# Two of the first loads on ScalarE's queue, small rows behind them, and the first norm shared between two engines

## Chip, cores and metric

One core of a Trainium2 chip runs the whole kernel. The metric is the device time of one execution in microseconds; lower is better.

## The reference, cut to what matters

A trunk of two layers on 256 tokens of width 1024, all in f32. Each layer norms x, modulates it by a vector made from `c`, projects it with `w_in`, runs two groups of attention heads, projects back and adds.

```python
cs = jax.nn.silu(c)
for l in range(DEPTH):                                   # DEPTH = 2
    mod = cs @ w_ada[l] + b_ada[l]                       # 1024 x 3072
    shift, scale, gate = split(mod, 3)
    h = rmsnorm(x, g_pre[l]) * (1.0 + scale) + shift     # x: 256 x 1024
    y = hybrid_mixer(h, w_in[l], w_out[l], ...)          # h @ w_in: 1024 x 3864
    x = x + gate * rmsnorm(y, g_post[l])

def rmsnorm(x, g):
    return x * lax.rsqrt(jnp.mean(x * x, axis=-1, keepdims=True) + 1e-6) * g
```

## The kernel before

x lies in two tiles `x[0]` and `x[1]` of 128 tokens by 1024 ("first half" and "second half" here). The first layer starts in an order written out by hand (`first_layer_start`, L793), behind which a scheduler orders the rest from `PLAN`. The start runs in five stages over the rows of the weights: `STAGES` gives for each the first block of 128 rows and how many (1, 1, 2, 2, 2). A stage needs the shift and scale of its rows, so it loads its own columns of `w_ada` and multiplies them with silu(c) on TensorE (`ada_on_pe`, L217), takes them out through ScalarE (`accr`, L246), turns them back (L253) and adds `b_ada` (`ada_cols`, L260). Then VectorE modulates x's transpose (L875), ScalarE and VectorE split it into a high and a low part (`hH` L878, `hL` L879), do the same with the weights (`hi` L365, `lo` L373), and TensorE multiplies three times for f32 (L858, L400 to L402).

The pieces of `w_ada` lie in tiles that are named for what they hold later: in stage 0 `qm` holds the 128 columns of shift and `km` those of scale, 512 KB each; then `qs`, `yH`, `yL` and again `qm`, `km`, `qs`, `yH`, `yL`. The weights of `w_in` lie in `raw`, a pool of seven buffers. All loads are issued on SP's queue in the order of the code. A load has one of eight semaphores in turn, and waits until the load eight places before it has landed.

x's way to the first projection: `square` on ScalarE with a sum beside it, in two halves of 512 columns (L310); `rstd` adds the two sums on VectorE (L304) and takes the power -0.5 on GpSimd (L306); `xhat_scale` multiplies on VectorE (L323), into a tile named `z` for the first half and `modG` for the second; TensorE transposes (`xt`, L832). On TensorE stand, in this order: matmuls with the identity (`warm`, L284, no part of the result), four transposes of `z`, `qm`'s matmuls, four transposes of `modG`, the transpose of the small rows `modrows` (`b_ada`, `g_pre`, `g_post`, L182), `km`'s matmuls.

Of the kernel before, what the change touches and what calls it, by code (L numbers as in the profile page):

```python
# [12 lines left out]
AF = mybir.ActivationFunctionType  # L13
OP = mybir.AluOpType
# [3 lines left out]
P = 128  # L18
S = 256
D = 1024  # L20
NT = S // P
# [47 lines left out]
class Trunk:  # L69
# [78 lines left out]
    def load_x_c(self):  # L148
        nc = self.nc
        self.c8 = self.cp.tile([KK, P], F32, name="c8")  # L150
        nc.sync.dma_start(self.c8, self.I["c"][0].rearrange("(k p) -> k p", p=P))
        self.x = []
        for t in range(NT):
            xt = self.cp.tile([P, D], F32, name=f"x{t}")
            nc.sync.dma_start(xt, self.I["x"][0, t * P:(t + 1) * P, :])
            self.x.append(xt)

    def silu_c(self):
# [27 lines left out]
        self.mb = mc  # L186
        self.mod = self.tl(self.mp, [P, 24], "mod", bufs=2)

    def ada_loads(self, l, spec, slots=None):

        wv = self.I["w_ada"][l].rearrange("(k p) c -> p k c", p=P)
        nk = UNIT // (spec[0][2] * P)
        units = []
        for u in range(KK // nk):
            for part, k0, n in spec:
                if slots:
                    raw = slots[len(units)].rearrange("p (k c) -> p k c", k=nk)
                else:
                    raw = self.tl(self.rp, [P, nk, n * P], "raw")
                c0 = part * D + k0 * P  # L200
                self.nc.sync.dma_start(raw, wv[:, u * nk:(u + 1) * nk, c0:c0 + n * P])
                units.append(raw)
        return units

# [588 lines left out]
    def first_layer_start(self):  # L793

        nc = self.nc
        l = 0
        wv = self.I["w_in"][l].rearrange("(k p) c -> p k c", p=P)
        tags = [("qm", 1), ("km", 1), ("qs0", 1), ("qs1", 1), ("yH", 2), ("yL", 2)]
        tags += tags
        spec = [[(0, k, n), (1, k, n)] for k, n in STAGES]  # L800

        def loads(s):
            k, n = STAGES[s]
            slots = []
            while len(slots) < 2 * n:
                tag, m = tags.pop(0)
                t = self.tl(self.mp, [P, m, UNIT], tag)
                slots += [t[:, i] for i in range(m)]
            ada = self.ada_loads(l, spec[s], slots)
            ks = slice(k, k + n)  # L810
            cols = [self.COLS_A0, [(O_KC, O_KS + 128), (O_KW, O_KW + 128)],
                    [(O_QN, O_QN + 512)], [(O_ZN, O_ZN + 256)]]
            return ada, [self.load([wv[:, ks, a:b] for a, b in c], n, sum(b - a for a, b in c))
                         for c in cols]

        self.load_mod_rows(0)
        ua, uw = loads(0)
        self.warm(WARM[0])
        self.silu_c()
        self.warm(WARM[1])  # L820
        xT = [self.tl(self.tp, [P, 4, S], "wide") for _ in range(2)]
        sq = [self.xhat_square(t, self.mp, ("z", "modG")[t]) for t in range(NT)]
        xh = [self.xhat_scale(t, h, self.rstd(ssq[:, 0:1], ssq[:, 1:2]))
              for t, (h, ssq) in enumerate(sq)]
        self.start_layer()
        pm = self.tl(self.ps, [P, 512], "av", bufs=1)

# [42 lines left out]
        for s, (k0, n) in enumerate(STAGES):  # L870
# [10 lines left out]
            if s + 1 < len(STAGES):  # L881
                ua, uw = loads(s + 1)
                on_dve = ON_VECTOR[s]
                if on_dve:
                    acc = self.ada_on_dve(spec[s + 1], ua[:on_dve])
# [166 lines left out]
```

## Time and profile before

| | |
|---|---|
| three timed runs, us | 343.06, 345.75, 345.78 (median 345.75) |
| profiled execution, us | 344.3, of which the span 342.6 |
| TensorE busy | 327.5 us, 96% |
| VectorE, ScalarE busy | 77%, 59% |

The span runs from the first to the last instruction that the profiler recorded. Busy shares are means over stages with different limits; the start of the kernel, where the change is, has to be read by itself.

### The profile page before, as it was taken

How to read it: one execution, taken by the hardware profiler on the slowest of the kernel's cores; microseconds unless marked ns; L12 is line 12 of the kernel's file. 1: busy time of each engine (PE TensorE's matmuls, PEld its weight loads, DVE VectorE, ACT ScalarE, POOL GpSimd, SP SyncE). 2: the span in 40 equal slices, each digit the busy share in tenths (PEclk: the TensorE clock that was granted, in tenths of full speed). 3: DMA queues.
4: the chain of work that ended last, by engine and by line, in shares of the span. 5: the costliest groups of instructions: out<-in, count | busy, mean ns of one | idle time of the engine just before them, and what ended most of it. 6: DMA issues, size and time to landing. Idle time of an engine off the chain costs nothing.

```text
span 342.6 us, 7585 instructions
## 1 busy us (share of the span) xinstructions
PE 327.5 (96%) x2852; PEld 294.5 (86%) x2852; DVE 264.8 (77%) x727; ACT 203.0 (59%) x506; POOL 10.2 (3%) x23
## 2 busy tenths in 40 slices
PE   8899989989999999989998999999999999999993
PEld 7689979989988887868998899998989889877992
DVE  2647686999998997878999968699899654796232
ACT  4423315866788985749376527471599935698311
POOL 2000000300000000000020100000000000000000
PEclk9999999999999999999999999999999999999999
DMA  7999999829985657699967698749557540000111
GB/s 236 317 319 355 349 346 262 237 64 330 348 275 182 223 191 239 196 312 371 284 173 226 184 200 243 214 166 346 185 162 260 194 125 0 2 0 3 64 62 61
DMA packets 72060, 71.12 MB, mean 208 GB/s; under 512 B 11440, under 2 KB 61784, under 8 KB 72024
## 3 DMA queue, kind: packets, MB, share of 16 engines
q1 hardware_dynamic: 72024, 70.65, 66.5%
q8 instruction: 22, 0.36, 0.4%
q14 instruction: 14, 0.11, 0.1%
HBM read 69.58 MB, written 1.06 MB: 206 GB/s over the span
## 4 chain that ended last, share of the span: by engine, by line
PE 68%; DVE 15%; DMA 8%; issue 4%; ACT 2%; POOL 1%; SPq 1%; DVEq 0%; POOLq 0%; ACTq 0%
PE pj L400 14%; PE pj L401 13%; PE pj L402 13%; PE tr L569 5%; DVE lo L373 4%; PE av L622 3%; DMA yL<-in_w_ada_dram 3%; PE tr L217 2%; PE sc L636 2%; DMA km<-in_w_ada_dram 2%; PE sc L604 2%; PE sc L605 2%; PE pj L858 2%; PE av L647 2%; DMA raw<-in_w_in_dram 2%
## 5 line engine op out<-in xcount | busy, mean ns | idle before, releaser
L373 DVE TENSOR_TENSOR lo<-raw,hi 128x1024 fp32r<-128x1024 f32 (+3 forms) x82 | 90.6, 1124 | 14.1 <-ACT hi L365 13.8
L400 PE MATMUL pj<-hH,lo 128*128 128x256 f32 x320 | 92.2, 288 | 0.0
L401 PE MATMUL pj<-hL,hi 128*128 128x256 f32 x320 | 91.4, 286 | 0.0
L402 PE MATMUL pj<-hH,hi 128*128 128x256 f32 x320 | 91.3, 285 | 0.0
L365 ACT CAST hi<-raw 128x1024 fp32r<-128x1024 f32 (+4 forms) x70 | 66.2, 966 | 18.3 <-PE pj L402 15.6
L400 PEld LDWEIGHTS pj<-hH,lo 128*128 128x128 f32 x320 | 61.1, 191 | 3.1 <-issue 2.3
L401 PEld LDWEIGHTS pj<-hL,hi 128*128 128x128 f32 x320 | 61.1, 191 | 1.3 <-issue 0.7
L402 PEld LDWEIGHTS pj<-hH,hi 128*128 128x128 f32 x320 | 61.1, 191 | 1.1 <-issue 0.6
L549 ACT ACTIVATE S<-S,mn 128x128 f32<-128x128 f32 (+1 forms) x96 | 42.8, 449 | 2.9 <-DVE mn L546 2.8
L234 DVE SCALAR_TENSOR_TENSOR acc<-raw,cs,acc 128x512 f32<-128x512 f32 x49 | 36.4, 744 | 2.0 <-DMA raw<-in_w_ada_dram 1.7
L546 DVE CUSTOM_DVE_ANT_0 S<-sc,bias 128x128 f32<-128x128 f32 (+1 forms) x96 | 30.9, 350 | 4.4 <-PE tr L569 2.6
L400 PE MATMUL pj<-hi,yL 128*128 128x256 f32 x112 | 31.8, 287 | 0.0
L402 PE MATMUL pj<-hi,yH 128*128 128x256 f32 x112 | 31.8, 285 | 0.0
L401 PE MATMUL pj<-lo,yH 128*128 128x256 f32 x112 | 31.7, 284 | 0.0
L575 ACT COPY PT<-tr 128x384 f32<-128x384 f32 x44 | 19.9, 480 | 12.8 <-PE tr L569 12.5
L400 PEld LDWEIGHTS pj<-hi,yL 128*128 128x128 f32 x112 | 20.9, 188 | 1.5 <-issue 1.3
L569 PE MATMUL tr<-ident,S 128*128 128x128 f32 x144 | 21.9, 278 | 0.2
L401 PEld LDWEIGHTS pj<-lo,yH 128*128 128x128 f32 x112 | 21.0, 188 | 0.6 <-issue 0.6
L402 PEld LDWEIGHTS pj<-hi,yH 128*128 128x128 f32 x112 | 21.1, 188 | 0.4 <-issue 0.4
L557 ACT ACTIVATE S<-S,sm 128x256 f32<-128x256 f32 (+1 forms) x46 | 20.2, 482 | 1.7 <-DVE sm L553 1.4
L549 ACT ACTIVATION_READ_ACCUMULATOR S<-S,mn 128x1 f32 x96 | 18.3, 191 | 0.0
L246 ACT COPY accr<-tr 128x128 f32<-128x128 f32 x12 | 3.2, 265 | 25.4 <-PE tr L241 18.4
(242 smaller groups left out, 626.5 us busy)
## 6 DMA issues: line engine op xcount, KB each, us to landing
raw<-in_w_in_dram SPq DMA_DIRECT2D x43, 512.0 KB, 4.7
raw<-in_w_ada_dram SPq DMA_DIRECT2D x32, 512.0 KB, 4.7
raw<-in_w_out_dram SPq DMA_DIRECT2D x16, 512.0 KB, 9.1
raw<-in_w_in_dram SPq DMA_DIRECT2D x9, 256.0 KB, 5.2
qs<-in_w_ada_dram SPq DMA_DIRECT2D x4, 512.0 KB, 8.8
yH<-in_w_ada_dram SPq DMA_DIRECT2D x4, 512.0 KB, 7.9
yL<-in_w_ada_dram SPq DMA_DIRECT2D x4, 512.0 KB
raw<-in_w_in_dram SPq DMA_DIRECT2D x9, 128.0 KB, 5.6
```

What stands on the lines that cost most here:

```text
L234: nc.vector.scalar_tensor_tensor(out=out, in0=raw[:, j], scalar=self.cs[:, k:k + 1], in1=out, op0=OP.mult, op1=OP.add)
L365: self.nc.scalar.copy(hi[:, :nk * n], raw[:, :nk * n])
L373: self.nc.vector.tensor_sub(lo[:, :nk * n], raw[:, :nk * n], hi[:, :nk * n].bitcast(F32))
L400: nc.tensor.matmul(out, aL, bH, start=first, stop=False)
L401: nc.tensor.matmul(out, aH, bL, start=False, stop=False)
L402: nc.tensor.matmul(out, aH, bH, start=False, stop=last)
L546: nc.vector.tensor_tensor_reduce(out=s[:, a:b], in0=sc[:, a:b], in1=self.bias[:, h, S - (b - a):S], scale=-1.0, scalar=3.0e38, op0=OP.add, ...
L549: nc.scalar.activation(s[:, a:b], s[:, a:b], AF.Exp, bias=mn[:, i:i + 1], scale=-1.0, accum_out=sm[:, i:i + 1])
L557: nc.scalar.activation(s[:, a:b], s[:, a:b], AF.Copy, scale=sm[:, i:i + 1]))
L569: mms += [nc.tensor.transpose(pt[:, i * P:(i + 1) * P], blk, self.ident) for i, blk in enumerate(blocks)]
L575: self.copies.append(nc.scalar.copy(ps, pt[:, :3 * P]))
L622: mms.append(nc.tensor.matmul(av[j * HD:(j + 1) * HD, kt * P:S], self.vsw[:, kt, vc], pts[j][:, kt * S:S + kt * P], start=False, stop=(i = ...
```

## The change

x's first half and `qm` are issued on ScalarE's queue, ahead of ScalarE's first other work; x's second half and `km` stay on SP. The three loads of `modrows` move behind `km`. x's second half is squared and summed on VectorE while ScalarE does the first half, and is scaled on ScalarE in place of VectorE; both `rstd` stand behind the squares.

```diff
--- before.py
+++ after.py
@@ -152,7 +152,7 @@
         self.x = []
         for t in range(NT):
             xt = self.cp.tile([P, D], F32, name=f"x{t}")
-            nc.sync.dma_start(xt, self.I["x"][0, t * P:(t + 1) * P, :])
+            (nc.sync if t else nc.scalar).dma_start(xt, self.I["x"][0, t * P:(t + 1) * P, :])
             self.x.append(xt)
 
     def silu_c(self):
@@ -186,7 +186,7 @@
         self.mb = mc
         self.mod = self.tl(self.mp, [P, 24], "mod", bufs=2)
 
-    def ada_loads(self, l, spec, slots=None):
+    def ada_loads(self, l, spec, slots=None, queues=None):
 
         wv = self.I["w_ada"][l].rearrange("(k p) c -> p k c", p=P)
         nk = UNIT // (spec[0][2] * P)
@@ -198,7 +198,8 @@
                 else:
                     raw = self.tl(self.rp, [P, nk, n * P], "raw")
                 c0 = part * D + k0 * P
-                self.nc.sync.dma_start(raw, wv[:, u * nk:(u + 1) * nk, c0:c0 + n * P])
+                queue = queues[len(units)] if queues else self.nc.sync
+                queue.dma_start(raw, wv[:, u * nk:(u + 1) * nk, c0:c0 + n * P])
                 units.append(raw)
         return units
 
@@ -806,22 +807,35 @@
                 tag, m = tags.pop(0)
                 t = self.tl(self.mp, [P, m, UNIT], tag)
                 slots += [t[:, i] for i in range(m)]
-            ada = self.ada_loads(l, spec[s], slots)
+            ada = self.ada_loads(l, spec[s], slots, None if s else (nc.scalar, nc.sync))
+            if s == 0:
+                self.load_mod_rows(0)
             ks = slice(k, k + n)
             cols = [self.COLS_A0, [(O_KC, O_KS + 128), (O_KW, O_KW + 128)],
                     [(O_QN, O_QN + 512)], [(O_ZN, O_ZN + 256)]]
             return ada, [self.load([wv[:, ks, a:b] for a, b in c], n, sum(b - a for a, b in c))
                          for c in cols]
 
-        self.load_mod_rows(0)
         ua, uw = loads(0)
         self.warm(WARM[0])
         self.silu_c()
         self.warm(WARM[1])
         xT = [self.tl(self.tp, [P, 4, S], "wide") for _ in range(2)]
-        sq = [self.xhat_square(t, self.mp, ("z", "modG")[t]) for t in range(NT)]
-        xh = [self.xhat_scale(t, h, self.rstd(ssq[:, 0:1], ssq[:, 1:2]))
-              for t, (h, ssq) in enumerate(sq)]
+        sq = [(self.tl(self.mp, [P, D], tag), self.tl(self.sp, [P, 2], "ssq"))
+              for tag in ("z", "modG")]
+        for half in range(2):
+            cs = slice(half * 512, (half + 1) * 512)
+            (h0, ssq0), (h1, ssq1) = sq
+            self.square(h0[:, cs], self.x[0][:, cs], ssq0[:, half:half + 1])
+            nc.vector.scalar_tensor_tensor(out=h1[:, cs], in0=self.x[1][:, cs], scalar=1.0 / D,
+                                           in1=self.x[1][:, cs], op0=OP.mult, op1=OP.mult,
+                                           accum_out=ssq1[:, half:half + 1])
+        rs = [self.rstd(ssq[:, 0:1], ssq[:, 1:2]) for h, ssq in sq]
+        xh = [h for h, ssq in sq]
+        self.xhat_scale(0, xh[0], rs[0])
+        for half in range(2):
+            cs = slice(half * 512, (half + 1) * 512)
+            nc.scalar.activation(xh[1][:, cs], self.x[1][:, cs], AF.Copy, scale=rs[1])
         self.start_layer()
         pm = self.tl(self.ps, [P, 512], "av", bufs=1)
 
```

On SP's queue, from the first load on, before (`c`, x, the small rows, `w_ada`, then `w_in`; a bracket names the semaphore that is waited for):

```order
L151 DMA c_95<-in_c_dram 8x128
L155 DMA x_97<-in_x_dram 128x1024
L155 DMA x_99<-in_x_dram 128x1024
L175 DMA modrows_104<-in_b_ada_dram 24x128
L175 DMA modrows_104<-in_g_pre_dram 8x128
L175 DMA modrows_104<-in_g_post_dram 8x128
L201 DMA qm_108<-in_w_ada_dram 128x8x128
L201 DMA km_109<-in_w_ada_dram 128x8x128
L357 DMA raw_112<-in_w_in_dram 128x128 [waits DMAHW0_49]
L357 DMA raw_112<-in_w_in_dram 128x152 [waits DMAHW1_49]
L357 DMA raw_112<-in_w_in_dram 128x232 [waits DMAHW2_49]
L357 DMA raw_116<-in_w_in_dram 128x384 [waits DMAHW3_49]
```

and now:

```order
L151 DMA c_95<-in_c_dram 8x128
L155 DMA x_99<-in_x_dram 128x1024
L202 DMA km_105<-in_w_ada_dram 128x8x128
L175 DMA modrows_108<-in_b_ada_dram 24x128
L175 DMA modrows_108<-in_g_pre_dram 8x128
L175 DMA modrows_108<-in_g_post_dram 8x128
L358 DMA raw_112<-in_w_in_dram 128x128 [waits DMAHW0_49]
L358 DMA raw_112<-in_w_in_dram 128x152 [waits DMAHW1_49]
L358 DMA raw_112<-in_w_in_dram 128x232 [waits DMAHW2_49]
L358 DMA raw_116<-in_w_in_dram 128x384 [waits DMAHW3_49]
L358 DMA raw_116<-in_w_in_dram 128x128 [waits DMAHW4_49]
L358 DMA raw_119<-in_w_in_dram 128x512 [waits DMAHW5_49]
```

`x_97` and `qm` are gone to ScalarE, and the small rows stand behind `km`. The loads of TensorE's first tiles show which load has which semaphore: now x's first half 0, `c` 1, x's second half 2, `qm` 3, `km` 4, the small rows 5 to 7; so the first `raw_116` waits for `qm` and the second for `km`, where before they waited for two of the small rows.

On SP's queue a little later, at the end of stage 1's weights (`raw_250` to `raw_259`) and the start of stage 2, before:

```order
L357 DMA raw_250<-in_w_in_dram 128x232 [waits DMAHW3_49]
L357 DMA raw_254<-in_w_in_dram 128x384 [waits DMAHW4_49]
L357 DMA raw_254<-in_w_in_dram 128x128 [waits DMAHW5_49]
L357 DMA raw_257<-in_w_in_dram 128x512 [waits DMAHW6_49]
L357 DMA raw_259<-in_w_in_dram 128x256 [waits DMAHW7_49,DVE_49,Activation_49]
L201 DMA yH_354<-in_w_ada_dram 128x4x256 [waits DMAHW0_49]
L201 DMA yH_354<-in_w_ada_dram 128x4x256 [waits DMAHW1_49]
L201 DMA yL_355<-in_w_ada_dram 128x4x256 [waits DMAHW2_49]
L201 DMA yL_355<-in_w_ada_dram 128x4x256 [waits DMAHW3_49]
```

and now, with loads that belong to the compression of the keys further on (`pe`, `w`):

```order
L358 DMA raw_250<-in_w_in_dram 128x232 [waits DMAHW3_49]
L358 DMA raw_254<-in_w_in_dram 128x384 [waits DMAHW4_49]
L358 DMA raw_254<-in_w_in_dram 128x128 [waits DMAHW5_49]
L358 DMA raw_257<-in_w_in_dram 128x512 [waits DMAHW6_49]
L436 DMA pe_892<-in_pe_k_dram 16x128 [waits DMAHW7_49]
L436 DMA pe_892<-in_pe_v_dram 16x128 [waits DMAHW0_49]
L465 DMA w_147_991<-in_w_ck_dram 64x64 [waits DMAHW1_49]
L466 DMA w_147_991<-in_w_ck_dram 64x64 [waits DMAHW2_49]
L467 DMA w_147_991<-in_w_cv_dram 64x64 [waits DMAHW3_49]
L358 DMA raw_259<-in_w_in_dram 128x256 [waits DMAHW4_49,DVE_49,Activation_49]
L202 DMA yH_354<-in_w_ada_dram 128x4x256 [waits DMAHW5_49]
L202 DMA yH_354<-in_w_ada_dram 128x4x256 [waits DMAHW6_49]
```

Five small loads, which stood some thirty places further back, have moved ahead of `raw_259` and `yH`, and `yH` waits for other loads than before.

On VectorE, between the last copy of `csz` (silu(c)) and the copies out of the transposes (`wide`), before:

```order
L169 COPY csz<-cs 128x8 [waits DVE_49]
L304 SCALAR_TENSOR_TENSOR rstd_157<-ssq_150 128x1 [waits Activation_49]
L323 TENSOR_SCALAR z_149<-x_97,rstd_157 128x512 [waits DMAHW1_49,Pool_49]
L323 TENSOR_SCALAR z_149<-x_97,rstd_157 128x512
L304 SCALAR_TENSOR_TENSOR rstd_162<-ssq_154 128x1 [waits Activation_49]
L323 TENSOR_SCALAR modG_153<-x_99,rstd_162 128x512 [waits DMAHW2_49,Pool_49]
L323 TENSOR_SCALAR modG_153<-x_99,rstd_162 128x512
L839 COPY wide_147<-tr_172 128x4x128 [waits PE_49]
L839 COPY wide_147<-tr_186 128x4x128 [waits PE_49]
```

and now:

```order
L169 COPY csz<-cs 128x8 [waits DVE_49]
L830 SCALAR_TENSOR_TENSOR modG_151,ssq_152<-x_99 128x512 [waits DMAHW2_49]
L830 SCALAR_TENSOR_TENSOR modG_151,ssq_152<-x_99 128x512
L305 SCALAR_TENSOR_TENSOR rstd_157<-ssq_150 128x1 [waits Activation_49]
L305 SCALAR_TENSOR_TENSOR rstd_160<-ssq_152 128x1 [waits DVE_49]
L324 TENSOR_SCALAR z_149<-x_97,rstd_157 128x512 [waits DMAHW0_49,Pool_49]
L324 TENSOR_SCALAR z_149<-x_97,rstd_157 128x512
L853 COPY wide_147<-tr_172 128x4x128 [waits PE_49]
L853 COPY wide_147<-tr_186 128x4x128 [waits PE_49]
```

The two scalings of `modG` are gone, two squares with a sum stand ahead of both `rstd`, and the `rstd` of the first half (`rstd_157`) so stands behind a wait for x's second half.

## Rows read from the trace of the kernel before

**Rows 1.** The page's totals and the granted clock in 40 slices.
```profile
PE 327.5 (96%) x2852; PEld 294.5 (86%) x2852; DVE 264.8 (77%) x727; ACT 203.0 (59%) x506; POOL 10.2 (3%) x23
...
PEclk9999999999999999999999999999999999999999
```

**Rows 2.** Timeline of the start: start us, us, engine line op, tiles [idle before <-releaser].
```profile
0.80 1.28 ACT L164 ACT_TABLE_LOAD   x1 [0.80 <-PEq L1038]
...
0.80 0.39 SPq L151 DMA_DIRECT2D c<-in_c_dram  x1
...
1.25 0.82 SPq L155 DMA_DIRECT2D x<-in_x_dram  x2
...
3.23 0.40 SPq L201 DMA_DIRECT2D qm<-in_w_ada_dram  x1
3.67 0.58 SPq L201 DMA_DIRECT2D km<-in_w_ada_dram  x1
...
4.48 0.63 ACT L310 ACTIVATE z<-x 128x512 f32<-128x512 f32 x1 [1.77 <-DMA x<-in_x_dram]
...
5.84 0.16 DVE L304 SCALAR_TENSOR_TENSOR rstd<-ssq 128x1 f32<-128x1 f32 x1 [2.52 <-ACT z L310]
...
6.67 0.88 DVE L323 TENSOR_SCALAR z<-x,rstd 128x512 f32<-128x512 f32 x2 [0.67 <-POOL rstd L306]
...
7.21 0.47 PEld L832 LDWEIGHTS tr<-ident,z 128*128 128x128 f32 x4
...
9.57 0.25 PE L182 MATMUL pj<-ident,modrows 40*128 40x40 f32 x1
...
10.22 1.07 PE L217 MATMUL av<-km,csz 128*32 128x128 f32 x16 [0.40 <-DMA km<-in_w_ada_dram]
...
16.34 1.99 SPq L201 DMA_DIRECT2D yH<-in_w_ada_dram  x2
```

**Rows 3.** Chain of waits in order of time: start us, us, what.
```profile
3.67 6.50 DMA km<-in_w_ada_dram
...
38.44 9.87 DMA yL<-in_w_ada_dram
...
54.52 0.74 DVE S L875 x2
...
145.50 5.49 DMA raw<-in_w_ada_dram
```

**Rows 4.** Waits of TensorE over the whole span: total us, times, longest us.
```profile
PE tr L217 <- DMA yL<-in_w_ada_dram: 1.5, 1, 1.5
```

**Rows 5.** By stretch: its us, busy us per engine, granted clock, DMA share, GB/s.
```profile
2.00:4.00 2.00, 1.99 (x10) 1.75 (x9) 0.51 (x3) 0.26 (x2) 0.00 (x0) 1.00 0.90 297
4.00:6.00 2.00, 2.00 (x12) 2.00 (x10) 0.16 (x1) 1.52 (x5) 0.00 (x0) 1.00 1.02 352
6.00:8.00 2.00, 1.93 (x17) 1.72 (x17) 0.95 (x4) 1.14 (x4) 0.85 (x2) 1.00 0.95 269
8.00:10.00 2.00, 1.82 (x21) 1.34 (x21) 1.71 (x4) 0.00 (x0) 0.26 (x1) 1.00 1.15 323
11.00:12.00 1.00, 0.63 (x9) 0.37 (x6) 0.00 (x0) 0.67 (x2) 0.00 (x0) 1.00 0.83 256
19.50:20.50 1.00, 1.00 (x11) 1.00 (x10) 0.86 (x3) 0.41 (x2) 0.00 (x0) 1.00 0.64 169
```

**Rows 6.** Waits of SP's queue, 0 to 60 us: total us, times, longest.
```profile
SPq L461 <- DVE lo L373: 4.7, 1, 4.7
...
SPq L201 <- DMA km<-in_w_ada_dram: 1.5, 1, 1.5
```

**Rows 7.** Timeline of SP's queue near 50 to 61 us, the small loads.
```profile
49.86 0.33 SPq L435 DMA_DIRECT2D pe<-in_pe_k_dram  x1
```

**Rows 8.** Groups by line and shape: count | busy us, mean ns | idle before.
```profile
L234 DVE SCALAR_TENSOR_TENSOR acc<-raw,cs,acc 128x512 f32<-128x512 f32 x49 | 36.4, 744 | 2.0 <-DMA raw<-in_w_ada_dram 1.7
...
L323 DVE TENSOR_SCALAR z<-x,rstd 128x512 f32<-128x512 f32 x2 | 0.9, 484 | 0.7 <-POOL rstd L306 0.7
```

## Prediction

> **What bounds the kernel now.** I read the page's totals first [rows 1]: TensorE is busy for 327.5 us, 96% of the span, so a change can give back only idle time of TensorE or time in which its work is padding; the clock is granted in full in all 40 slices, so nothing here turns on it. The change touches the first 12 us, so next I read that stretch instruction by instruction [rows 2]. Three things meet there. The x path: x's first half is there at 4.48 (ScalarE starts squaring), rstd starts at 5.84, GpSimd's power holds VectorE until 6.67, and TensorE transposes from 7.21. The modulation path: `qm` (the first piece of w_ada, for shift) is consumed behind these transposes, `km` (the second, for scale) from 10.22. Between the two TensorE has 0.4 us of true idle time, since the rows of `modrows` end at 9.82; ahead of it stand matmuls that need x and `qm`. The last matmul of `km` ends at 11.29, and the first projection follows from it.
>
> The chain of waits says what comes behind [rows 3]: `km`'s transfer for 6.5 us, then TensorE, and at 38.44 another transfer, the modulation weights of the fifth stage (`yL`), for 9.87 us. TensorE stands 1.5 us for it [rows 4]. From 2 us on the DMA engines are busy 0.9 to 1.15 of the time at 270 to 350 GB/s [rows 5], and all loads of this part are one stream on SP's queue. So **the first 48 us end when the load stream ends**, and a later TensorE start is first eaten by that 1.5 us. From 54.5 VectorE is on the chain [rows 3], so the shift that the stream leaves is handed on.
>
> **DMA issues.** x's first half goes from SP's second place (1.25) to ScalarE's first. ScalarE and SP are both released at 0.80 [rows 2], so its issue comes 0.45 us earlier, x's second half 0.4 earlier, `qm` about 2 us earlier (3.23 to 1.3), `km` about 2 earlier (3.67 to 1.7). The bytes are the same: x 1049 KB, the two pieces 1049 KB, rows and c 24 KB, 2.12 MB in all. By the rates of rows 5 these had passed at 8.85 before (1840 KB by 8.0, then 323 GB/s) while `km` was taken as landed at 10.22: the last engine and the signal trail the bytes by 0.7 (x's first half: 524 KB passed at 3.76, landed 4.48) to 1.35 us. With a start 0.45 earlier they pass at about 8.2 and both pieces land at 8.4 to 9.2. For `km` that is 1.0 to 1.8 us sooner. For `qm` no row has two queues at once: its lower end is its own time before (at most 4.7 us after issue: TensorE took it at 7.9 without a wait), so 6.0; the upper end is `km`'s. I take the upper end, 8.4 to 8.8, since the engines are already full [rows 5] and now serve x's second half and `km` on the other queue in the same stretch. The Trainium skill, DMA: Bandwidth & Descriptors, section Issuing engines are not separate DMA queues, says that transfers started on several engines run on the same 16 engines and interleave, so that only issue time is saved; by it the upper end holds, and no row of this kernel shows it.
>
> ScalarE pays two issues of 0.4 us [rows 2] ahead of its table load (0.80 to about 1.65). The load then ends at 2.95 in place of 2.1, tanh waits some 0.4, `csz` is ready at about 3.6: hidden, as nothing reads it before `qm` lands.
>
> **A wait that the order shows.** At most eight transfers are under way: each transfer takes the semaphore of the one eight before it and waits for that one to land. Before, SP could issue all seven weight pieces of stage 0 (896 KB) ahead of `km`'s landing and then stood 1.5 us for `km` [rows 6]. Now the fourth piece (`raw_116`) needs the semaphore of `qm`, the fifth that of `km`, and the next three those of the small rows behind `km`. Only 256 KB are queued when `qm` lands. These take 0.8 us at 330 GB/s; landing trails by 0.7 to 1.35, and a new issue needs about 1.0 us to its first bytes (issue of x 1.25, no rate to speak of before 2.0 [rows 2, 5]). So the engines run dry for 0.9 to 1.55 us near 8.5 to 10. Before, the corresponding hole (11 to 12, 256 GB/s against 340) cost 0.25. Net loss 0.65 to 1.3 against 0.45 (and, of the slow 2 to 4 us, 297 GB/s against 352, some 0.2) gained: 0 to +0.65, I take **+0.3**.
>
> The second place: five small loads (`pe` twice, `w` three times) stood near 50 to 61 us on SP and now stand among the pieces of stage 1, ahead of `raw_259` and `yH`. Each holds one of the eight semaphores and 0.33 us of SP at the least [rows 7]. `yH`'s first piece, released by `qs`'s second landing and issued at 16.34 before [rows 2], now waits for a `raw_254` piece: about 18.0. Some 770 KB are queued then, which ends about when the new bytes would come: 0 to 1.2 us dry, against 0.5 lost before in 19.5 to 20.5 (169 GB/s [rows 5]). I take **+0.3**, ends -0.5 and +0.7. That they are gone from 50 to 61 I cost at nothing: VectorE is full there, and SP itself waited 4.7 us for it [rows 6].
>
> **The x path.** Squares of the first half stay on ScalarE (two of 0.62 and two reads of 0.19 [rows 2]), those of the second go to VectorE beside them. No row has this VectorE form with a sum beside it; the nearest is 744 ns for 128x512 with two f32 inputs [rows 8]. Below is its own tensor-scalar scaling, 484, above is two passes, 1.4 us. I take 0.7 each. But VectorE does them ahead of rstd of the first half, so that rstd now waits for x's second half: landed at 5.0 to 5.6, middle 5.3 (before by 5.8, when ScalarE turned to it without a wait), plus 1.45, is 6.75 in place of 5.84. From there the old distances hold: 1.37 to the transposes (8.1), then 3.75 for transposes 0.7, `qm`'s matmuls 1.1 (as `km`'s), transposes 0.65, rows 0.2, `km`'s 1.09. Second-half scaling on ScalarE (2 x 0.62, from about 8.2) is ready when TensorE gets there at 9.9. End of `km`'s matmuls: **11.85 in place of 11.29**. By `qm`'s landing the same sum gives 8.4 to 8.8 plus 3.0, 11.4 to 11.8. So the earlier `km` buys nothing: TensorE starts its projections 0.1 to 0.7 us later, which the 1.5 us at 48 swallow. Cost 0, and that much if the stream were on time and the wait shorter.
>
> The Trainium skill, Vector Engine (DVE) Microarchitecture Reference, section Points that are easy to get wrong, says that this operation with two sources that are not bf16 and an accumulator runs at half rate. By it a square takes some 1.3 us, an estimate, and the projections start 1.2 us later still; the row without a sum (744 ns) is the nearer bound, no row has the sum.
>
> **Sum.** 0.3 + 0.3 + 0 = +0.6 us on the profiled execution's 344.3 (span 342.6 and 1.7 around it). The three timed runs lie at 343.06 to 345.78; the four executions have a mean of 344.7, the median is 345.75. I set no change at 345.3, between them, and forecast **345.9**. One per cent, 3.5 us, is about what a measurement here tells from no change; the runs spread by 0.8%.
>
> **Rivals.**
> *Faster start* (0.18): `qm` lands at 6 to 7 and x's second half at 4.9, so both chains meet at 11.0 and the holes close under the bytes still queued. Gain 0.45 + 0.2 in the stream and a little of the hole of 11 to 12: -1.0, 344.3. For: the old single queue had a hole at its start. Against: the engines were 0.9 busy already in 2 to 4 us [rows 5], so an earlier issue adds few bytes.
> *Slower, by the eight transfers* (0.17): both holes at their far ends, 1.3 + 0.7, and the fifth stage's `yL` late by 2.0: 347.3. It decides if `yH`'s first piece is issued after 18.3, because `yL`'s pieces for the third stage, issued behind it, then come late for TensorE as well.
> *Half-rate squares* (0.05): two passes over the inputs, 1.4 us each by the 744 ns row, so rstd at 8.15 and `km`'s end at 13.2, 1.9 later than before, 0.4 beyond the wait at 48; SP's buffers come free later as well, up to 0.6 more on the forecast: 346.5.
> *It does not do what it says* (0.07): `km` lands no earlier than 9.7, as the weights behind it run along; the wait for it lasts longer and so does the hole: 346.4.
> *The rest in another order* (0.16): behind the start the scheduler has moved instructions on every engine (small loads, casts, matmuls). Nothing there was meant; a late transfer such as the one at 145.5, on the chain for 5.49 us [rows 3], can turn by up to 2: 343.3 or 347.3, evenly.
> Forecast as summed: 0.37.
>
> The range reaches from 343.0 to 348.6: the rivals' ends, and the spread of the runs. Faster by over 1% (below 342.3) needs two rivals at once and a low run: 0.10; slower (above 349.2) the same: 0.10; within: 0.80.
>
> **What would show it.** Right: SP stands idle before the fourth `raw` until `qm` has landed, some 2 us; DMA rate drops below 200 GB/s between 8.5 and 10; VectorE's rstd at about 6.75, TensorE's transposes at about 8.1, last `km` matmul at about 11.85 with no wait for `km`; five small issues near 16 to 18; the wait for `yL` at 48 shorter, and its end at 48.5 to 49. Wrong: squares well off 0.7 us; `qm` in before 7.5; no dip in the rate; `yL` in by 47.8; or a difference that starts only behind 80 us.

## The result, and the profile after

The changed kernel takes 348.17 us (median of 4 runs, 347.92 to 350.0), the kernel before 345.16 (4 runs beside it, 343.06 to 345.78). The ratio is 1.0117, 95% interval 1.0076 to 1.0158: **1.2% slower**, 3.0 us by the medians and 4.0 by the ratio, where +0.6 was forecast. Ratios, here and below, leave out executions with a disturbed clock, medians don't, so that the two need not agree where such runs were many. The profiled execution took 348.18, of which the span is 346.5.

The page of the changed kernel, its totals and the granted clock, in answer to [rows 1]:

```profile
PE 330.4 (95%) x2852; PEld 296.9 (86%) x2852; DVE 265.9 (77%) x729; ACT 203.2 (59%) x504; POOL 10.3 (3%) x23
...
PEclk9998999999999999999999899999999999999998
```

The work is the same, but the clock is no longer full in all slices: the fourth slice (26 to 35 us) shows a dip, so does the 23rd (190 to 199 us), and so does the last. The first of them lies 15 us behind the edited steps. The dips do not make the loss: of the four timed executions two had a mean granted clock of 0.998 and 0.996 and took 348.16 and 347.92 us, the two with 0.987 (the profiled one) and 0.988 took 348.18 and 350.0.

Timeline of the changed kernel's start, as [rows 2]:

```profile
0.80 0.40 ACTq L155 DMA_DIRECT2D x<-in_x_dram  x1
...
1.22 0.49 ACTq L202 DMA_DIRECT2D qm<-in_w_ada_dram  x1
...
1.66 0.42 SPq L202 DMA_DIRECT2D km<-in_w_ada_dram  x1
...
5.82 0.69 DVE L830 SCALAR_TENSOR_TENSOR modG<-x 128x512 f32<-128x512 f32 x1 [2.00 <-DMA x<-in_x_dram]
6.44 0.08 DVE L830 DVE_READ_ACCUMULATOR modG<-x 128x1 f32 x1
...
7.05 0.28 DVE L305 SCALAR_TENSOR_TENSOR rstd<-ssq 128x1 f32<-128x1 f32 x2
...
8.41 0.66 PE L846 MATMUL tr<-ident,z 128*128 128x128 f32 x4 [0.72 <-DVE z L324]
9.00 1.07 PE L218 MATMUL av<-qm,csz 128*32 128x128 f32 x16
...
10.77 1.07 PE L218 MATMUL av<-km,csz 128*32 128x128 f32 x16
```

The edited part does what was forecast of it: squares of 0.69 us, rstd at 7.05 (forecast 6.75), transposes at 8.41 (8.1), the last matmul of `km` at 10.77 + 1.07 = 11.84 (11.85), with no wait for `km`. SP's queue a little later (the same view, SP alone) is where the two kernels part:

```profile
10.66 1.06 SPq L202 DMA_DIRECT2D qs<-in_w_ada_dram  x2
11.76 6.27 SPq L358 DMA_DIRECT2D raw<-in_w_in_dram  x6
18.08 0.43 SPq L436 DMA_DIRECT2D pe<-in_pe_k_dram  x1
18.55 0.42 SPq L436 DMA_DIRECT2D pe<-in_pe_v_dram  x1
19.01 0.55 SPq L465 DMA_DIRECT2D w<-in_w_ck_dram  x1
19.61 0.59 SPq L466 DMA_DIRECT2D w<-in_w_ck_dram  x1
20.24 0.59 SPq L467 DMA_DIRECT2D w<-in_w_cv_dram  x1
20.96 0.50 SPq L358 DMA_DIRECT2D raw<-in_w_in_dram  x1
21.51 0.99 SPq L202 DMA_DIRECT2D yH<-in_w_ada_dram  x2
```

From 18.08 to 20.96 SP issues five loads that bring 64 KB together (two of 8 KB, three of 16 KB). The diff does not name them; the scheduler has put them there. In the order of the built programs all five come forward only with both loads on ScalarE's queue; with one of the two moved just the two `pe` do; neither of these was run. The five issues alone take 2.58 of the 2.88 us, and the waits of SP's queue list no landing between 11 and 23 us, so that here the loads cost their turns and no wait. And `yH`, issued at 16.34 before [rows 2], goes out at 21.51. The changed kernel by stretches (us of it, busy us per engine, granted clock, DMA share, GB/s) shows what that does:

```profile
16.00:20.00 4.00, 4.00 (x51) 3.58 (x50) 0.60 (x2) 1.34 (x3) 0.00 (x0) 1.00 0.83 243
20.00:24.00 4.00, 3.89 (x27) 3.28 (x26) 3.73 (x10) 1.86 (x4) 0.35 (x1) 1.00 0.47 123
24.00:28.00 4.00, 1.94 (x26) 1.59 (x28) 0.13 (x1) 0.00 (x0) 0.00 (x0) 0.86 1.07 363
28.00:32.00 4.00, 4.00 (x49) 3.23 (x45) 0.00 (x0) 0.00 (x0) 0.00 (x0) 0.72 1.11 341
```

The kernel before moved 308 and 339 GB/s in the first two of these stretches, had TensorE busy for all of the third, and the full clock in all four:

```profile
16.00:20.00 4.00, 4.00 (x54) 3.67 (x53) 0.90 (x6) 1.13 (x3) 0.00 (x0) 1.00 0.99 308
20.00:24.00 4.00, 4.00 (x47) 3.47 (x48) 2.96 (x7) 1.75 (x4) 0.35 (x1) 1.00 1.01 339
24.00:28.00 4.00, 4.00 (x52) 3.32 (x49) 0.04 (x1) 0.27 (x1) 0.00 (x0) 1.00 1.12 342
```

Waits of TensorE from 14 to 60 us, in answer to [rows 4]:

```profile
PE tr L218 <- DMA yH<-in_w_ada_dram: 2.2, 2, 1.5
...
PE tr L218 <- DMA yL<-in_w_ada_dram: 0.4, 1, 0.4
```

A wait for `yH` of 2.2 us is new, and the wait for the fifth stage's `yL` has shrunk from 1.5 to 0.4. The chain of waits (start us, us, what), in answer to [rows 3]:

```profile
21.99 5.09 DMA yH<-in_w_ada_dram
...
43.43 8.64 DMA yL<-in_w_ada_dram
...
58.29 0.74 DVE S L889 x2
```

`yL` now lands at 52.07 in place of 48.31, and VectorE begins to modulate for the fifth stage at 58.29 in place of 54.52. I call that start **the milestone**. It lies 3.77 us later; the rest of the span lasts 288.2 us (346.5 - 58.29), before 288.1. In the two profiled executions the whole loss therefore lies ahead of the milestone. But the rest lasts anything from 286.8 to 290.4 us in the profiled executions below that keep the order of one of these two kernels, so this agreement says little about the rest. The milestone is the sharper instrument for the start, and the timed runs are for the whole.

### The profile page after: what moved, and what is told of

Same layout as the page of the kernel before. It is cut to its first block, busy times and chain, and to the rows that moved or that the text cites. A ratio compares the mean times of both kernels' runs of the same rounds, so it can differ in the third digit from the quotient of the medians.

```text
span 346.5 us, 7572 instructions
## 1 busy us (share of the span) xinstructions
PE 330.4 (95%) x2852; PEld 296.9 (86%) x2852; DVE 265.9 (77%) x729; ACT 203.2 (59%) x504; POOL 10.3 (3%) x23
## 3 DMA queue, kind: packets, MB, share of 16 engines
HBM read 69.58 MB, written 1.06 MB: 204 GB/s over the span
## 4 chain that ended last, share of the span: by engine, by line
PE 69%; DVE 16%; DMA 7%; issue 3%; ACT 3%; POOL 1%; SPq 0%; DVEq 0%; POOLq 0%; ACTq 0%
PE pj L401 14%; PE pj L402 14%; PE pj L403 13%; DVE lo L374 5%; PE tr L570 5%; PE tr L218 3%; PE av L623 3%; DMA yL<-in_w_ada_dram 2%; PE sc L637 2%; PE av L648 2%; PE sc L605 2%; PE sc L606 2%; DMA yH<-in_w_ada_dram 1%; DMA raw<-in_w_in_dram 1%; DVE wide L743 1%
## 5 line engine op out<-in xcount | busy, mean ns | idle before, releaser
L550 ACT ACTIVATION_READ_ACCUMULATOR S<-S,mn 128x1 f32 x96 | 18.3, 191 | 0.0
```

Source lines behind the costliest of these rows:

```text
L550: nc.scalar.activation(s[:, a:b], s[:, a:b], AF.Exp, bias=mn[:, i:i + 1], scale=-1.0, accum_out=sm[:, i:i + 1])
```

## Experiments

The theory: five small loads, which have moved ahead of `raw_259` and `yH`, keep SP from putting large transfers on their way; the DMA engines run dry, and the load stream, which sets the end of the start, is late by as much. Rivals: the hole behind `qm` near 10 us, x's new path, and the scheduler's other order behind the start. In the diffs `small` stands for the two loads of `pe` and the three of `w` of layer 0, taken out of their functions and called at the place shown.

All runs in one table. "Order" says whose order of instructions TensorE follows behind the start. Ratios are to the kernel before on the same chip (medians 344.84, 343.93 and 344.81 for the runs 1 to 4, 5 to 8 and 9 to 12).

| kernel | order | median us | ratio, 95% | `yH` issued | milestone |
|---|---|---|---|---|---|
| before | before | 345.16 | 1 | 16.34 | 54.52 |
| changed | after | 348.17 | 1.0117 (1.0076 to 1.0158) | 21.51 | 58.29 |
| 1 changed, small behind the start | other | 353.21 | 1.0167 (1.0084 to 1.025) | 17.02 | 54.70 |
| 2 before, five small early | after | 347.63 | 1.0106 (1.007 to 1.0143) | 19.30 | 56.12 |
| 3 before, small behind the start | other | 352.19 | 1.022 (1.0163 to 1.0277) | 16.26 | 53.44 |
| 4 as 1, rows first | other | 350.39 | 1.0175 (1.0107 to 1.0243) | 16.53 | 54.35 |
| 5 changed, small on GpSimd | after | 345.61 | 1.0033 (1.0003 to 1.0064) | 17.71 | 54.76 |
| 6 before, small on GpSimd | after | 345.63 | 1.0035 (1.0004 to 1.0067) | 16.44 | 53.70 |
| 7 as 5, rows first | after | 345.23 | 1.002 (0.9991 to 1.005) | 16.80 | 53.88 |
| 8 as 5, x's old path | after | 346.99 | 1.0076 (1.0042 to 1.0109) | 17.77 | 54.74 |
| 9 before, two small early | before | 345.48 | 1.0027 (0.9994 to 1.006) | 16.82 | 54.68 |
| 10 before, eight small early | after | 349.48 | 1.0149 (1.0122 to 1.0176) | 21.35 | 58.64 |
| 11 changed, rows first, small behind the start | before | 345.16 | 1.0023 (0.9996 to 1.0051) | 17.09 | 54.75 |
| 12 before, small behind the start, rows of layer 1 on GpSimd | before | 344.51 | 1.0013 (0.9986 to 1.0041) | 16.36 | 53.72 |

**1. The changed kernel without the early small loads.**

```diff
+        self.small0 = self.load_pe(0), self.load_w2(0)   # behind the start's last load
+        self.load_mod_rows(1)
```

> The changed kernel, with the small loads of the compression (pe, w of layer 0) and the next layer's three small rows issued by hand behind the last weights of stage 4, so that none stands among the loads of stage 1. Theory 1 (the five small loads hold semaphores and SP's turns, and so dry the DMA engines in 18 to 23 us): the second hole goes, yL of the fifth stage lands near 49.5 in place of 52.1, 345.8 to 346.5 us, some 2 us below the changed kernel. Theory 2 (it is the hole of 9.5 to 14 us behind the semaphores of qm and km): no more than 0.7 us better, 347.5 to 348.2. Theory 3 (the later x path): no gain, 348.2. TensorE's clock should read full in 24 to 32 us if its fall only followed TensorE's wait for yH.

The milestone came back to 54.70, 3.59 us earlier than in the changed kernel; 20 to 24 us moved 317 GB/s, TensorE never waited for `yH`, and the clock stayed full from 24 to 32 us. But the whole was 1.67% slower than the kernel before, where 345.8 to 346.5 us had been expected.

**2. The kernel before with the five small loads early**, on the old start, between `raw_257` and `raw_259`.

```diff
+                if s == 1 and i == 3:
+                    self.small0 = self.load_pe(0), self.load_w2(0)
```

> The kernel before, with the five small loads put by hand where the changed kernel has them, between raw_257 and raw_259 of stage 1; all else as before. Theory 1: the second hole appears by itself, TensorE waits for yH, 347 to 348 us. Theory 2 and 3: 345.2, as before, or 0.5 above.

On the old start, too, the five loads make a hole (153 GB/s from 16 to 20 us), and this kernel is 1.06% slower. Not all of that is the hole: behind the start TensorE follows the changed kernel's order here, and run 6, with that order and without a hole, costs 0.35%. So some 0.7%, or 2.4 us, is left for the hole. SP's queue of this run:

```profile
14.61 0.43 SPq L433 DMA_DIRECT2D pe<-in_pe_k_dram  x1
16.02 0.33 SPq L433 DMA_DIRECT2D pe<-in_pe_v_dram  x1
16.39 0.55 SPq L439 DMA_DIRECT2D w<-in_w_ck_dram  x1
16.99 1.00 SPq L440 DMA_DIRECT2D w<-in_w_ck_dram  x1
18.03 0.60 SPq L441 DMA_DIRECT2D w<-in_w_cv_dram  x1
18.76 0.50 SPq L357 DMA_DIRECT2D raw<-in_w_in_dram  x1
```

Between the first and the second `pe` SP waits (1.0 us by the waits of its queue) until `qs` has landed. This wait is not an extra cost of the small loads: run 6, which has none here, stands 1.4 us for the same landing, ahead of `yH`. What a small load costs is its turn, 0.33 to 0.60 us and once 1.00 here. `raw_259` goes out at 18.76, where the same start without them (run 6) issues it at 14.71.

**3. Control for 1:** the kernel before with the same two lines as 1.

> A control for e1: the kernel before with the same small loads by hand at the end of the start. All theories: within 0.7 us of the kernel before, 344.5 to 345.9; what it shows beyond that is the price of the tool itself.

The control failed: 2.2% slower, though its milestone is the earliest of all (53.44). With these lines the scheduler gives everything behind the start another order than either kernel has, and that order costs 5 to 10 us (351.3 - 53.44 = 297.9 us behind the milestone, against 288.1). The total times of 1, 3 and 4 therefore say nothing on the change; what lies ahead of their milestones does.

**4. As 1, with layer 0's small rows ahead of `km`.**

```diff
-            if s == 0:
-                self.load_mod_rows(0)
...
+        self.load_mod_rows(0)
         ua, uw = loads(0)
```

> As e1, and the rows of modrows issued ahead of km again, so that stage 0's weights wait for x, c and the rows and only qs waits for km. Theory 2: the first hole goes too, and with both gone the earlier start shows: 344.5 to 345.5, 1 us or more below e1. Theory 1 alone: as e1, within 0.4 us. Theory 3: as e1, the x path still ends at 11.8.

`qs` went out at 9.28, `yH` at 16.53 in place of run 1's 17.02, and the milestone at 54.35: 0.35 earlier.

**5 and 6. The same small loads on GpSimd's queue**, behind its two powers, in the changed kernel (5) and in the kernel before (6); layer 1's rows go with them. Both follow the changed kernel's order behind the start, on TensorE instruction by instruction.

```diff
-            self.nc.sync.dma_start(pe[16 * i:16 * i + 16, :],
+            (self.nc.sync if l else self.nc.gpsimd).dma_start(pe[16 * i:16 * i + 16, :],
...
+        self.small0 = self.load_pe(0), self.load_w2(0)
+        self.load_mod_rows(1)
```

> The changed kernel; only the small loads (pe and w of layer 0, the three small rows of layer 1) are issued on GpSimd's queue behind its two powers, so that none stands on SP and none takes one of SP's eight semaphores. The instructions of TensorE, VectorE and ScalarE stand in the changed kernel's order. Theory 1 (small loads): the second hole goes, the fifth stage's modulation on VectorE starts near 55.5 in place of 58.3, and as the rest takes 288.2 us in both kernels, 345.3 us. Theory 2 (first hole decides): starts at 57.5 or later, 347.5 us. Theory 3 (x path): 348.

> The control: the kernel before with the same small loads on GpSimd, with the changed kernel's order behind the start. Theories 1 to 3: start of the fifth stage at 53.5 to 54.5, rest 288.2, so 343.5 to 345. Should the order behind the start have cost the changed kernel its time, this run is slow too, 347 or more.

Run 5 is the cleanest test: start, order and bytes of the changed kernel; only the queue of the small loads differs, and with it their moment (layer 1's rows come along). GpSimd issues them early too:

```profile
8.30 0.71 POOL L434 DMA_DIRECT2D pe<-in_pe_k_dram  x1
9.00 0.51 POOL L434 DMA_DIRECT2D pe<-in_pe_v_dram  x1
...
10.54 0.52 POOL L442 DMA_DIRECT2D w<-in_w_cv_dram  x1
```

Issued there, the 64 KB cost nothing that shows: `yH` goes out 3.80 us earlier than in the changed kernel, and the milestone is 54.76, 3.53 us ahead of it:

```profile
17.71 1.10 SPq L202 DMA_DIRECT2D yH<-in_w_ada_dram  x2
...
54.76 0.74 DVE L899 TENSOR_SCALAR S<-wide,mod 128x256 f32<-128x256 f32 x2
```

The time is 345.61, 0.8% less (1.0117 against 1.0033). Run 5's stretch in which the changed kernel moves 123 GB/s:

```profile
20.00:24.00 4.00, 4.00 (x33) 3.47 (x33) 3.72 (x10) 1.75 (x4) 0.34 (x1) 1.00 1.04 357
```

So it is the place on SP's queue that costs, not the transfers. Run 6 came 0.6 us above the upper end that I had set for it (345.63 against 345). Beside run 5 its 1.0035 says that the changed start as such costs nothing that these runs can time (345.61 against 345.63), although its stream is later: `yH` 1.27 us, the milestone 1.06.

**7. As 5, with layer 0's rows ahead of `km`** (the diff of 4).

> As e5, with the small rows ahead of km again: stage 0's weights no longer wait for km and the rows behind it, all but the last can be issued ahead of qm's landing. Theory 2: a gain of 1 us against e5. Theory 1: the first hole is a matter of 0.4 us, as e1 against e4 showed at the fifth stage (54.70 and 54.35).

`qs` was issued at 9.26 in place of 10.63, 8 to 16 us moved 303 GB/s in place of 257 (the kernel before: 311), and the milestone is 53.88: the hole behind `qm` and `km` exists and costs the stream 0.9 us. Of these the timed runs show 0.4 (345.61 to 345.23), less than the intervals are wide and less than the 1 us of theory 2.

**8. As 5, with x's old path** (squares of both halves on ScalarE, both scalings on VectorE).

```diff
+        sq = [self.xhat_square(t, self.mp, ("z", "modG")[t]) for t in range(NT)]
+        xh = [self.xhat_scale(t, h, self.rstd(ssq[:, 0:1], ssq[:, 1:2]))
+              for t, (h, ssq) in enumerate(sq)]
```

> As e5, with x's second half squared on ScalarE and scaled on VectorE as before. Theory 3: back by 1 us or more against e5. Theories 1 and 2: within 0.3 us of e5, since the load stream ends the start and not the x path; the projections of stage 0 may start a little earlier than 14.06.

TensorE transposes at 7.06 in place of run 5's 8.56, then stands 0.9 us for `qm`, and its projections start 0.7 us earlier (13.64 against 14.37). The milestone does not move (54.74 against 54.76): x's path is hidden behind the stream, as forecast. The total is 1.4 us longer all the same, where 0.3 at most was expected; that lies behind the milestone (290.1 us against 287.7), and its cause is open.

**9 and 10. The dose:** two and eight small loads at the place of run 2.

```diff
+                    self.small0 = (self.load_pe(0),)                                          # 9
+                    self.small0 = self.load_pe(0), self.load_w2(0); self.load_mod_rows(1)     # 10
```

> The kernel before with only the two pe loads issued between the fifth and the sixth of the first stage's loads; the three w loads stay where they were, and so does the order of everything behind the start. Theory (each small load costs one turn of the SyncE queue, in which nothing new is put on its way: 2.4 us for five, so about 0.5 each): the fifth stage's modulation starts on VectorE 1.0 us later than in the two runs of this start without early small loads (53.70 and 54.52), so at 54.7 to 55.5, and the time is 0.5 to 1 us above the kernel before. Rival (the loss is that of one refused turn or of the bunch as a whole, whatever their number): 56.1, as with five, and 2 us above.

> The kernel before with eight small loads at that place: the two pe, the three w and the next layer's three rows. Theory (a turn of about 0.5 us each): the fifth stage's modulation starts at 53.7 + 8 x 0.5, 57.7 to 58.5, and TensorE waits for yH longer than the 1.0 us seen with five; the time is 3.5 to 4 us above the kernel before, with the 0 to 1 us that this order behind the start costs included. Rival (the loss does not grow with the number): 56.1, and 2 us above.

Milestones on the old start: 53.70 and 53.72 with none (runs 6 and 12), 54.68 with two, 56.12 with five, 58.64 with eight: 0.5 us for each of the first five, 0.84 for the last three. The kernel before itself, which has none either, came at 54.52; against it the delays would be 0.16, 1.60 and 4.12 us. With either base the loss grows with the number, and the rival that the number does not matter is out. The timed runs agree: each against the control of its own order (run 9 against 12, runs 2 and 10 against 6), the ratios put two, five and eight loads at some 0.5, 2.4 and 3.9 us. Run 10 came above what was expected of it, in the milestone (58.5 at the most) and in the time (1.49%, some 5 us, where 3.5 to 4 were expected). TensorE's waits in run 10:

```profile
PE tr L217 <- DMA yH<-in_w_ada_dram: 3.3, 2, 2.8
```

With five on this start it had been 1.0, with two none. Run 10 by stretches, as above:

```profile
16.00:18.00 2.00, 2.00 (x37) 1.67 (x36) 0.00 (x0) 0.80 (x3) 0.00 (x0) 1.00 0.84 269
18.00:20.00 2.00, 2.00 (x19) 2.00 (x18) 1.10 (x5) 0.22 (x2) 0.00 (x0) 1.00 0.13 32
20.00:22.00 2.00, 2.00 (x15) 1.87 (x14) 1.86 (x5) 1.27 (x3) 0.34 (x1) 1.00 0.12 25
22.00:24.00 2.00, 0.66 (x3) 0.19 (x1) 0.92 (x2) 0.40 (x1) 0.00 (x0) 1.00 0.87 244
```

These four rows are 2 x (269 + 32 + 25 + 244) = 1140 KB. Run 12, with none, moved 2676 KB in the same eight microseconds. The 1536 KB that are missing take 4.5 us at 340 GB/s; the milestone is 4.92 us late. The same sum for the other runs (sums of the stretches from 16 to 24 us; the changed kernel against run 5, the others against run 12):

| kernel | KB from 16 to 24 us | missing KB | at 340 GB/s, us | milestone late by, us |
|---|---|---|---|---|
| 9, two small | 2316 | 360 | 1.1 | 0.96 |
| 2, five small | 1830 | 846 | 2.5 | 2.40 |
| 10, eight small | 1140 | 1536 | 4.5 | 4.92 |
| changed, five small | 1464 | 1228 | 3.6 | 3.53 |

**The milestone is late by the bytes that the hole left out**, here to within 0.5 us. Counted from the start to 24 us, and against run 12, the same sum takes in the first hole as well and holds for every kernel of the table to within 0.6 us: the changed kernel is short of 1606 KB, 4.7 us, and 4.57 late; run 5 of 283 KB, 0.8 us, and 1.04 late.

**11 and 12. A version meant to have neither hole, and its control:** 11 is the change with layer 0's rows ahead of `km`, the small loads behind the start and layer 1's rows on GpSimd; 12 is the kernel before with the last two of these.

```diff
-            self.nc.sync.dma_start(self.rows[a:b, :],
+            (self.nc.gpsimd if l else self.nc.sync).dma_start(self.rows[a:b, :],
...
+        self.small0 = self.load_pe(0), self.load_w2(0)   # behind the start's last load
```

> The change without either hole: x's first half and qm on ScalarE's queue and the squares on VectorE as in the changed kernel, the three rows of the first layer ahead of km as before, the small loads on SyncE behind the start's loads, the next layer's rows on GpSimd's queue; the order behind the start is that of the kernel before. Theory (the change's loss lies in the two holes alone, and a faster start of x is worth nothing since TensorE waits for weights): the fifth stage's modulation starts at 53.7 to 54.5, the time is that of the kernel before within 0.5%. Rival (the new path of x gives back its 0.3 us or more once the holes are gone): milestone below 53.5, 0.3 to 0.5% faster than before.

> Control of the last one: the kernel before with the same place for the small loads and the next layer's rows on GpSimd's queue; the order behind the start is that of the kernel before. Theory: the time of the kernel before within 0.3%, milestone 53.7 to 54.5. Rival (that the next layer's rows sit on GpSimd's queue costs something by itself, as in the pair with all small loads there): 1 us or more slower.

This time the order behind the start is that of the kernel before, and the control holds: 1.0013 (0.9986 to 1.0041). Run 11 gives 1.0023 (0.9996 to 1.0051): what is left of the change, x's new path and the earlier loads, is worth nothing that these runs can time, and no version here beats the kernel before. A small hole is left, though: 247 GB/s from 16 to 20 us, where run 12 moves 328. Its milestone, 54.75, is 0.25 above the upper end that I expected, though run 7 with the same start came at 53.88. So a milestone by itself is good to about 0.9 us between executions (before and run 12, which have the same start, differ by 0.8; against its own control, run 12, run 11 is 1.03 late), and differences under 1 us, the hole behind `qm` among them, rest on `yH`'s issue and on the rates rather than on it.

## Why the prediction was wrong

The forecast was 345.9 with a range of 343.0 to 348.6; the measured median is 348.17. That median by itself lies inside the range; by the ratio, 1.17% on the 345.3 that I had set for no change, it is 349.3, outside. The sign of the sum was right and the size not: +0.6 forecast, 1.17% (4 us) measured, beyond the 1% to which I gave 8 chances in 10.

**The step that failed is "The second place", the five small loads: "I take +0.3, ends -0.5 and +0.7".** It measured 3.53 us at the milestone (58.29 against run 5's 54.76) and 2.9 us in the timed ratio (1.0117 against 1.0033, 0.84% of 345). Three numbers in it were too kind:

- "Each holds one of the eight semaphores and 0.33 us of SP at the least": I priced the least. The five took 18.08 to 20.96, 2.88 us, 0.58 each; the row of 0.33 [rows 7] is one of a `pe`, and the `w` take 0.55 to 0.59.
- `yH`'s first piece was to go out at "about 18.0". At 18.08 SP had only come to the first small load; `yH` went out at 21.51. Of the 5.17 us of delay, 1.27 come from the changed start (runs 5 and 6) and 3.80 from the five loads (changed and run 5), the other 0.1 is the difference between run 6 and the kernel before.
- "Some 770 KB are queued then": the changed kernel moved 150 and 233 GB/s in the two microseconds from 18 on, 383 KB in all, and then 24 and 31 GB/s for two more. What is queued shrinks while SP is held up, and I had not followed it to the moment at which the small loads come up. The last of its six `raw` issues alone lasts from 16.42 to 18.03, with no wait listed; in the kernel before the two pieces of `yH` are the slow ones, 1.99 us [rows 2]. Why an issue takes so long there is open.

**The rival that came true** is "Slower, by the eight transfers" (0.17), with its place and its point of decision: `yH` after 18.3. In the table no run with `yH` at 17.77 or earlier has a milestone above 54.76, and all three with 19.30 and later have 56.12 to 58.64. Its price, 347.3, was bounded by the same +0.7 and so 0.9 us short of the median. TensorE stood for `yH` itself (2.2 us), ahead of the `yL` that the rival names.

**The first hole** ("0 to +0.65, I take +0.3"): the dip below 200 GB/s between 8.5 and 10 came (77 GB/s from 9.5 to 10), SP stood 2.6 us for `qm`. In the stream it cost 0.9 us (run 7) to 1.27 (run 5 against 6, `yH`), more than the upper end; in the time nothing to 0.4 us. Why so little of it reaches the time is not shown; TensorE's wait for `yL` does not take it in (0.8 us in run 5, 0.6 in run 6).

**The loads.** `qm` landed 7.5 us after its issue at 1.22, at 8.7, `km` 7.7 us after 1.66, at 9.4: the upper end that I took (8.4 to 8.8) for `qm`, and the "about 2 earlier" of `km`'s issue bought 0.8 us of its landing (10.17 before, 3.67 plus 6.50 [rows 3]), less than the "1.0 to 1.8" forecast. The rule of the Trainium skill, DMA: Bandwidth & Descriptors, section Issuing engines are not separate DMA queues, that a second issuing engine saves only the time to issue, agrees: side by side with `qm` on the other queue, `km` took 7.7 us to land in place of 6.50. It calls that saving usually small; for five small loads in SP's way, the changed kernel and run 5 put it at 2.9 us.

**x's path.** The end of `km`'s matmuls, 11.84 where 11.85 was forecast, was hit by luck: x's second half landed at 5.80 (1.25 plus 4.55), beyond the 5.0 to 5.6 allowed, the two squares took 1.23 us in place of 1.45, and from the transposes to that end it was 3.43 in place of 3.75. The 1.36 from rstd to the transposes was right, and run 8 shows that the path is hidden. The half-rate rule of the Trainium skill, Vector Engine (DVE) Microarchitecture Reference, section Points that are easy to get wrong, is not borne out: 0.69 us for 128x512 with two f32 inputs and a sum, and 0.08 for the read of the sum, no more than the 744 ns of the form without a sum [rows 8]; the measurement decides.

**What stays open.** Of the 1.17%, 0.84 are the five loads. The rest, some 0.35% or 1.2 us, is what run 6 (1.0035, interval 1.0004 to 1.0067) costs with the old start and the new order behind it, while run 12 with the old order costs 0.13%, interval across zero. The two intervals overlap. But of the executions with a mean granted clock of 0.995 or more, run 6's six have a mean of 345.7 us against 343.9 for the kernel before beside it (23 executions), and run 12's six 343.9 against 344.0 (16). So some 1 to 2 us beside the five loads are real, and they point to the rival "The rest in another order". It is not shown as the cause: run 6 also has the small loads on GpSimd, and the profiles of single executions vary by as much behind the milestone.

## What to carry to other kernels

Where one queue feeds a stream that sets the end, price an extra load on it by the queue's time to issue it and by the bytes that could have gone out in that time, not by its own bytes: five loads of 64 KB in all cost 3.5 us here, and 1228 KB not moved explain them. After any edit of loads look where the scheduler has put loads that the edit does not name, at each place work out what is still under way when they come up, and price the turns from rows of those very loads. An earlier issue is worth little while the bytes ahead of it fill the engines: by 8 us the kernels with the new start had moved some 100 KB more than those with the old one, 0.3 us' worth, and the hole behind `qm` took that back.

## What was not expected of the hardware

**The clock follows a standstill of TensorE.** In the changed kernel TensorE is busy for 1.94 of the 4 us from 24 to 28, mostly waiting for `yH`. Its stretches of 2 us:

```profile
26.00:28.00 2.00, 1.37 (x20) 0.99 (x17) 0.00 (x0) 0.00 (x0) 0.00 (x0) 0.71 1.07 356
28.00:30.00 2.00, 2.00 (x14) 1.56 (x11) 0.00 (x0) 0.00 (x0) 0.00 (x0) 0.50 1.14 329
30.00:32.00 2.00, 2.00 (x36) 1.67 (x35) 0.00 (x0) 0.00 (x0) 0.00 (x0) 0.93 1.09 353
```

A granted clock of 0.50 is the lower level, 1.2 in place of 2.4 GHz. Run 10, with 3.3 us of waiting, shows the same (0.50 from 28 to 30); run 2, with 1.0 us for `yH` and 1.31 busy of 2 us, stays at 1.00 in this part. The slower matmuls cost nothing visible there: the missing bytes account for the milestone. Nor does the dip come each time: the three stretches above would by themselves bring the mean granted clock down to 0.995, and the timed executions of the changed kernel at 0.998 and 0.996 took no less time.

**A short wait of TensorE was followed by a dip in one execution and not in another**, of two kernels with the same order behind the start. Run 8 is busy for 0.42 of the 2 us from 184 to 186 and then has 0.50 from 188 to 190; run 5, busy for 0.52 of the same 2 us, keeps 1.00. The first of these rows is run 8's, 188 to 190:

```profile
188.00:190.00 2.00, 2.00 (x11) 2.00 (x11) 2.00 (x4) 1.11 (x4) 0.31 (x1) 0.50 0.06 16
```

and this is run 5's:

```profile
188.00:190.00 2.00, 2.00 (x19) 2.00 (x18) 2.00 (x4) 1.27 (x5) 0.41 (x1) 1.00 0.05 13
```

In those 2 us TensorE gets 11 matmuls recorded in place of 19. That may be one reason why single executions differ behind the milestone; no run tested it. It is not what makes run 8 slower than run 5 in the timed runs: with a mean granted clock of 0.995 or more run 8's five executions have a mean of 346.9 us, run 5's seven 345.3.
